# The recurrence chain's products for both heads at once, over 128 columns

## Chip, cores, metric

The kernel runs on one core of one Trainium2 chip. The metric is the device time of one execution in microseconds (us). The core's engines are TensorE (PE in the profile, its weight loads PEld), VectorE (DVE), ScalarE (ACT), GpSimd (POOL) and SyncE (SP).

## What is computed

The reference is a backbone of two layers over 512 latent and 256 context tokens of width 1024. Each layer has a mixer (differential attention, a bidirectional RWKV-7 recurrence and a short convolution, with gates) and a mixture of 16 experts. What matters here is the recurrence, run for 8 heads of size 64 in both directions, first over the context and then over the latent tokens, from the context's state:

```python
def step(s, inp):
    wt, kkt, at, kt, vt = inp[:5]
    sa = jnp.einsum('bhvk,bhk->bhv', s, kkt)
    s = s * wt[:, :, None, :] - sa[..., None] * (kkt * at)[:, :, None, :] + vt[..., None] * kt[:, :, None, :]
    y = jnp.einsum('bhvk,bhk->bhv', s, inp[5]) if emit else None
    return s, y
```

In the second layer the context's outputs y are not needed.

## The kernel before

The recurrence is done in chunks of 64 tokens. Two heads make a pair (128 partitions), so there are 4 pairs, and of each 12 chunks: 4 of the context, 8 of the latent tokens. The two directions `d` are done side by side. `rwkv_phase` runs through pairs and chunks of a layer, and for each chunk calls two things.

`window` prepares a chunk three calls ahead, with nothing of the state: products of keys and rates (`kbd`, `cbd`, `kr`), the masked matrices `g.sv`, `g.sc`, `g.tok`, and by six levels of fp16 products (`nb`, `wt`, `xx`, `xt`) an approximate inverse `g.xt`. DVE's part of a level is `wt` (L736), ACT's are `xx` and `xt` (L753, L757).

`chain` (L771) takes the state and goes through the chunk in a row of dependent steps. The tile `V` holds for each head and direction the state on 64 partitions and the value rows on the other 64; the two heads have them on opposite halves. Per call:

1. the right-hand side `zz`: `g.sv` times `V`, each head by itself, two directions summed, into that head's 64 partitions of the bank `pz`;
2. `zr`, a copy of `zz` (ACT, L806), and `aa`, `g.xt` times `zr`;
3. `sa`, a copy of `aa` (L812), and `zz` again, with `g.sc` times `sa` added;
4. `zr` as `zz` less `sa` (DVE, L804), and `aa` once more, with `g.xt` times `zr` added;
5. `aa` copied into the value rows' place in `V`, a head at a time (DVE, L824), and `pss`, the next state: `g.tok` times `V`, each head by itself, into the bank `py`;
6. the next chunk's `V` from `pss` and the decayed state `sf`, a head at a time (DVE, L846; L848 at a pair's first chunk).

Where outputs are wanted (`emit`), `yy` is made beside this, `g.sv` times `V` for each head and `g.sc` times `sa`, and copied out (ACT, L854). So a product of one head has 64 weight columns and writes 64 partitions:

```python
for h, hs in enumerate(halves):
    first = self.mma(zz[hs, 0], g.sv[:, 0, h, 0], V[:, 0, h], True)
    with tc.issue_after(first.ins):
        self.mma(zz[hs, 1], g.sv[:, 1, h, 0], V[:, 1, h])
```

All matmuls of the chain are recorded at L85 (`mma`), nearly all others at L81 (`mm`). Between the chain's steps the program places other work, doled out by `fill`: the projections `pw` (weights split in a high and a low part), three matmuls of 512 or 256 columns a step, and `pa`. It gives the chain the highest priority, then the windows, then this fill. The order on each engine is then set by a scheduler that follows a timeline of its own, and every engine goes through its own list strictly in order.

Of the kernel before, what the change touches and what calls it, by code (L numbers as in the profile page):

```python
# [8 lines left out]
F32 = mybir.dt.float32  # L9
# [58 lines left out]
class Trunk:  # L68
# [570 lines left out]
    def window(self, q, n, emit, kb):  # L639
# [39 lines left out]
        for h in range(2):  # L679
            hs, ho = slice(64 * h, 64 * h + 64), slice(64 - 64 * h, 128 - 64 * h)  # L680
            v.tensor_tensor(kbd[hs, :, ho], two(q.k)[hs], t1[hs], ALU.mult)
            v.scalar_tensor_tensor(cbd[hs, :, hs], kk[hs], -1.0, t2[hs], ALU.mult, ALU.mult)
            dst = g.sv[hs, :, h, :nm]
            if n:
                f = q.f[hs, :, n - 1, None, None].to_broadcast([64, 2, nm, 64])
                nc.gpsimd.tensor_tensor(dst, kr[hs, :, :nm], f, ALU.mult)
            else:
                nc.gpsimd.tensor_copy(dst, kr[hs, :, :nm])
# [9 lines left out]
        for h in range(2):  # L698
            ho = slice(64 - 64 * h, 128 - 64 * h)
            v.tensor_tensor(g.sv[ho, :, h, :nm], ps[ho, 0, :, :nm], self.scc[ho, :, :nm], ALU.mult)  # L700
# [70 lines left out]
    def chain(self, q, n, V, emit):  # L771
# [19 lines left out]
        pz = self.psz.tile([P, 2, 2, HD], F32, name="pz", tag="z")  # L791
        zz, aa = pz[:, 0], pz[:, 1]
        self.mark()
        for h, hs in enumerate(halves):
            first = self.mma(zz[hs, 0], g.sv[:, 0, h, 0], V[:, 0, h], True)
            with tc.issue_after(first.ins):
                self.mma(zz[hs, 1], g.sv[:, 1, h, 0], V[:, 1, h])
        py = self.psz.tile([P, 2, 2, HD], F32, name="py", tag="y")
        pss, yy = py[:, 0], py[:, 1]
        sa = None  # L800
        for it in range(2):
            r = rp.tile([P, 2, HD], F32R, name="zr", tag="zr", bufs=2)
            if it:
                v.tensor_tensor(r, zz, sa, ALU.subtract)  # L804
            else:
                nc.scalar.activation(r, zz, AF.Copy)  # L806
# [3 lines left out]
            if not it:  # L810
                sa = rp.tile([P, 2, HD], F32, name="sa", tag="sa", bufs=2)
                nc.scalar.activation(sa, aa, AF.Copy)  # L812
                self.mark()
                for d in range(2):
                    self.mma(zz[:, d], g.sc[:, d, 0], sa[:, d])
                if emit:

                    firsts = []
                    for h, hs in enumerate(halves):
                        firsts.append(self.mma(yy[hs, 0], g.sv[:, 0, h, 1], V[:, 0, h], True))  # L820
                        with tc.issue_after(firsts[-1].ins):
                            self.mma(yy[hs, 1], g.sv[:, 1, h, 1], V[:, 1, h])
        for h, hs in enumerate(halves):
# [5 lines left out]
        for h, hs in enumerate(halves):  # L829
            if last:  # L830
                break
            if emit:
                with tc.issue_after(firsts[h].ins):
                    for d in range(2):
                        self.mma(pss[hs, d], g.tok[:, d, h], V[:, d, h])
            else:
                first = self.mma(pss[hs, 0], g.tok[:, 0, h], V[:, 0, h], True)
                with tc.issue_after(first.ins):
                    self.mma(pss[hs, 1], g.tok[:, 1, h], V[:, 1, h])
        if emit:  # L840
            for d in range(2):
                self.mma(yy[:, d], g.sc[:, d, 1], sa[:, d])
        if not last:
            for h, hs in enumerate(halves):
                if n:
                    v.tensor_tensor(out[hs, :, h], pss[hs], sf[hs], ALU.add)  # L846
                else:
                    v.tensor_copy(out[hs, :, h], pss[hs])  # L848
        if emit:
# [4 lines left out]
            nc.scalar.activation(ysl, yy, AF.Copy)  # L854
# [1081 lines left out]
```

## Time and profile before

| | us |
|---|---|
| median of 3 runs | 3746.64 |
| lowest, highest | 3741.66, 3747.3 |
| the profiled execution | 3755.7 |
| its span in the trace | 3753.9 |
| the recurrence phase of the first layer, about | 115 to 975 |
| the recurrence phase of the second layer, about | 2170 to 2870 |

The profile is of one execution. The page gives the busy time of each engine, and further views split it by stretch, by group of instructions, by wait, or show the instructions in order of time. A record of PE lasts longer than the time to the next one, since matmuls overlap: what a matmul costs is read from start to start. Each matmul on plain fp32 operands has two records. A form such as 128*64 128x64 f32 reads: 128 rows and 64 columns of the array, the operand that streams through has 128 partitions and 64 columns. A wait is named by the instruction that was waited for last.

### The profile page before, as it was taken

The page shows a single profiled execution, that of the slowest core. Times are in us where ns is not written, and L with a number is a line of the kernel's source. Part 1 is how long each engine was busy: PE and PEld are TensorE (multiplying, and loading weights), DVE is VectorE, ACT ScalarE, POOL GpSimd, SP SyncE. Part 2 cuts the span into 40 slices and gives each one's busy share as a digit, 9 for nine tenths or more (in the row PEclk, how much of TensorE's full clock was granted, in tenths as well). Part 3 has the DMA queues.
Part 4 walks back from the last instruction along what each step waited for, and adds up shares of the span by engine and source line. Part 5 has one row for each costly group of instructions (what it writes and reads, how often), then busy time and mean ns, then how long its engine had stood idle before and what let it go on. Part 6 is the DMA issues. An engine that isn't in the chain of part 4 may idle for free. (4 is left out here: it accounts for less than half of the span.)

```text
span 3753.9 us, 58688 instructions
## 1 busy us (share of the span) xinstructions
PE 3485.4 (93%) x22479; PEld 2313.5 (62%) x22479; DVE 2025.0 (54%) x4902; ACT 1284.2 (34%) x3145; POOL 893.0 (24%) x1181
## 2 busy tenths in 40 slices
PE   6999999999998998999999899899999989799998
PEld 4777777777987892233333467677777978633442
DVE  6787878773665461121222677878773766412122
ACT  3454444443444211111110344555553452211111
POOL 3333343332320420000000243334343312100000
PEclk9999999999999998999999899898999999899999
DMA  5312031334115435778888411111112135399998
GB/s 177 102 61 95 29 111 49 110 114 150 52 39 183 136 133 211 294 293 310 331 331 328 138 57 29 31 36 38 35 38 92 46 132 186 132 409 409 409 409 351
DMA packets 297053, 621.11 MB, mean 165 GB/s; under 512 B 19258, under 2 KB 160532, under 8 KB 296772
## 3 DMA queue, kind: packets, MB, share of 16 engines
q1 hardware_dynamic: 293028, 605.30, 44.5%
q0 software_dynamic: 1728, 6.29, 0.5%
q10 hardware_dynamic: 2016, 5.77, 0.4%
q8 instruction: 177, 2.90, 0.3%
q14 instruction: 104, 0.85, 0.1%
HBM read 584.00 MB, written 33.29 MB: 164 GB/s over the span
## 5 line engine op out<-in xcount | busy, mean ns | idle before, releaser
L81 PE MATMUL ph<-we,xin 128*64 128x512 f32 x2048 | 514.8, 607 | 7.7 <-DMA we<-in_exp_w 4.7
L81 PE MATMUL pw<-hhi,w_hi 128*128 128x512 f32 (+1 forms) x1272 | 500.0, 397 | 14.5 <-ACT w_hi L132 6.3
L81 PE MATMUL pw<-hlo,w_hi 128*128 128x512 f32 (+1 forms) x1272 | 457.3, 364 | 0.0
L81 PE MATMUL pw<-hhi,w_lo 128*128 128x512 f32 (+1 forms) x1272 | 455.9, 364 | 1.0 <-POOL w_lo L134 1.0
L134 POOL TENSOR_TENSOR w_lo<-w_raw,w_hi 128x1024 fp32r<-128x1024 f32 x124 | 302.3, 2444 | 413.4 <-ACT w_hi L132 340.9
L81 PEld LDWEIGHTS ph<-we,xin 128*64 128x64 f32 x2048 | 151.5, 139 | 330.5 <-issue 315.7
L736 DVE TENSOR_TENSOR wt<-slot,lvm 128x256 f16<-128x256 f32 x576 | 232.8, 418 | 114.3 <-PE slot L81 78.8
L81 PEld LDWEIGHTS pw<-hhi,w_hi 128*128 128x128 f32 x1272 | 245.5, 195 | 55.2 <-ACT w_hi L132 7.6
L81 PEld LDWEIGHTS pw<-hhi,w_lo 128*128 128x128 f32 x1272 | 244.9, 194 | 38.9 <-issue 3.8
L81 PEld LDWEIGHTS pw<-hlo,w_hi 128*128 128x128 f32 x1272 | 246.2, 195 | 32.8 <-issue 13.8
L132 ACT ACTIVATE w_hi<-w_raw 128x1024 fp32r<-128x1024 f32 x168 | 177.1, 1057 | 239.4 <-DMA w_raw<-in_w_in 63.3
L81 PE MATMUL py<-we,hT 128*64 128x512 f32 x1024 | 248.5, 607 | 8.0 <-DMA we<-in_exp_w 2.8
L1791 POOL TENSOR_TENSOR ylo<-y,yhi 128x512 fp32r<-128x512 f32 x28 | 35.3, 1280 | 891.6 <-ACT yhi L1790 891.6
L753 ACT ACTIVATE xx<-slot 128x256 f16<-128x256 f32 x384 | 145.7, 382 | 166.0 <-PE slot L81 154.2
L1801 DVE TENSOR_TENSOR xr<-xr,psc 128x512 f32<-128x512 f32 x144 | 90.3, 682 | 196.6 <-PE psc L81 196.4
L1718 ACT ACTIVATE sl<-ph 64x512 f32<-64x512 f32 x64 | 37.8, 590 | 451.5 <-PE ph L81 431.8
L1719 DVE TENSOR_TENSOR hid<-sl,ph 64x512 f32<-64x512 f32 x64 | 44.2, 690 | 267.2 <-ACT sl L1718 266.7
L81 PE MATMUL slot<-xt,wt 128*128 128x128 f16 x960 | 135.9, 229 | 34.8 <-DVE wt L736 34.3
L81 PEld LDWEIGHTS py<-we,hT 128*64 128x64 f32 x1024 | 70.2, 137 | 151.6 <-issue 132.7
L81 PE MATMUL pt<-w_hi,hhi 128*128 128x256 f32 x544 | 156.2, 289 | 4.8 <-ACT xk L1115 2.0
L768 POOL COPY V<-vt 64x128 f32<-64x128 f32 x192 | 58.1, 305 | 425.3 <-PE py L85 323.0
L81 PE MATMUL pt<-w_lo,hhi 128*128 128x256 f32 x544 | 155.7, 287 | 3.2 <-POOL w_lo L134 3.2
(418 smaller groups left out, 7779.9 us busy)
## 6 DMA issues: line engine op xcount, KB each, us to landing
we<-in_exp_w SPq DMA_DIRECT2D x384, 1024.0 KB
w_raw<-in_w_in SPq DMA_DIRECT2D x124, 512.0 KB
ada_w<-in_ada_w SPq DMA_DIRECT2D x96, 512.0 KB
w_raw<-in_w_branch SPq DMA_DIRECT2D x24, 512.0 KB
w_raw<-in_w_out SPq DMA_DIRECT2D x20, 512.0 KB
gd<-gt SPq DMA_DIRECT2D x24, 384.0 KB
g<-gd SPq DMA_DIRECT2D x24, 384.0 KB
gd<-gt SPq DMA_DIRECT2D x24, 256.0 KB
```

The lines of the kernel that those rows point to most:

```text
L81: return self.leg(self.nc.tensor.matmul(out, lhsT, rhs, start=start, stop=stop))
L132: nc.scalar.activation(hi, raw, AF.Copy)
L134: self.lo_eng.tensor_tensor(lo, raw, hi.bitcast(F32), ALU.subtract)
L736: v.tensor_tensor(wt, ps, self.lvm[:, :, l], ALU.mult)
L753: nc.scalar.activation(x, ps2, AF.Copy)
L768: self.nc.gpsimd.tensor_copy(t[ho, :, h], self.two(q.vt[s][ho], z0, z1))
L1718: nc.scalar.activation(sl, ph[0:64, ns], AF.Silu)
L1719: v.tensor_tensor(hid[0:64, ns], sl, ph[64:128, ns], ALU.mult)
L1791: (v if by_block else self.ylo_eng[nh]).tensor_tensor(lo, yn, hi.bitcast(F32), ALU.subtract)
L1801: v.tensor_tensor(x, x, pt, ALU.add)
```

## The change

The two heads' weights are laid side by side in `g.sv` (the head's index moves to the last place but one; `g.tok` lies so already), so that one matmul has 128 weight columns, and the moving operand is `V` of both heads, 128 columns. The result holds for each head's 64 partitions the product with both heads' values; only the blocks of a head with itself are read. The products with `g.sc` must add into the same layout, so they read `sa` twice (`both`). `pz` and `py` become a bank each. What copies `zz`, `pss` and `yy` out reads one head's block at a time: the first copy of `zz` is split between ACT and DVE, the subtraction is two on DVE, the copy of `yy` two on ACT.

```diff
--- before.py
+++ after.py
@@ -680,7 +680,7 @@
             hs, ho = slice(64 * h, 64 * h + 64), slice(64 - 64 * h, 128 - 64 * h)
             v.tensor_tensor(kbd[hs, :, ho], two(q.k)[hs], t1[hs], ALU.mult)
             v.scalar_tensor_tensor(cbd[hs, :, hs], kk[hs], -1.0, t2[hs], ALU.mult, ALU.mult)
-            dst = g.sv[hs, :, h, :nm]
+            dst = g.sv[hs, :, :nm, h]
             if n:
                 f = q.f[hs, :, n - 1, None, None].to_broadcast([64, 2, nm, 64])
                 nc.gpsimd.tensor_tensor(dst, kr[hs, :, :nm], f, ALU.mult)
@@ -697,7 +697,7 @@
                 self.mm(ps[:, t, d, :nm], lhs[:, d], kr[:, d, :nm], True, True)
         for h in range(2):
             ho = slice(64 - 64 * h, 128 - 64 * h)
-            v.tensor_tensor(g.sv[ho, :, h, :nm], ps[ho, 0, :, :nm], self.scc[ho, :, :nm], ALU.mult)
+            v.tensor_tensor(g.sv[ho, :, :nm, h], ps[ho, 0, :, :nm], self.scc[ho, :, :nm], ALU.mult)
         hi = lambda t: t.rearrange("p d m (h i) -> p d m h i", h=2)[:, :, :nm]
         if emit:
             hi = lambda t: t.rearrange("p d m (h i) -> p (d m) h i", h=2)
@@ -788,22 +788,34 @@
                     sf[hs], V[hs, :, h], fc[hs, :, None].to_broadcast([64, 2, HD]), ALU.mult
                 )
 
-        pz = self.psz.tile([P, 2, 2, HD], F32, name="pz", tag="z")
-        zz, aa = pz[:, 0], pz[:, 1]
+
+        own = list(enumerate(halves))
+        both = lambda t, d: t[:, d, None].to_broadcast([P, 2, HD])
+        pz = self.psz.tile([P, 512], F32, name="pz", tag="z")
+        zz = pz[:, 0:256].rearrange("p (d h x) -> p d h x", d=2, h=2)
+        aa = pz[:, 256:384].rearrange("p (d x) -> p d x", d=2)
+        py = self.psz.tile([P, 2, 2, 2, HD], F32, name="py", tag="y")
+        pss, yy = py[:, 0], py[:, 1]
+
+        def begin(out, lhs):
+
+            first = self.mma(out[:, 0], lhs(0), V[:, 0], True)
+            with tc.issue_after(first.ins):
+                self.mma(out[:, 1], lhs(1), V[:, 1])
+            return first
+
         self.mark()
-        for h, hs in enumerate(halves):
-            first = self.mma(zz[hs, 0], g.sv[:, 0, h, 0], V[:, 0, h], True)
-            with tc.issue_after(first.ins):
-                self.mma(zz[hs, 1], g.sv[:, 1, h, 0], V[:, 1, h])
-        py = self.psz.tile([P, 2, 2, HD], F32, name="py", tag="y")
-        pss, yy = py[:, 0], py[:, 1]
-        sa = None
+        begin(zz, lambda d: g.sv[:, d, 0])
+        sa = first = None
         for it in range(2):
             r = rp.tile([P, 2, HD], F32R, name="zr", tag="zr", bufs=2)
-            if it:
-                v.tensor_tensor(r, zz, sa, ALU.subtract)
-            else:
-                nc.scalar.activation(r, zz, AF.Copy)
+            for h, hs in own:
+                if it:
+                    v.tensor_tensor(r[hs], zz[hs, :, h], sa[hs], ALU.subtract)
+                elif h:
+                    v.tensor_copy(r[hs], zz[hs, :, h])
+                else:
+                    nc.scalar.activation(r[hs], zz[hs, :, h], AF.Copy)
             self.mark()
             for d in range(2):
                 self.mma(aa[:, d], g.xt[:, d], r[:, d])
@@ -812,46 +824,41 @@
                 nc.scalar.activation(sa, aa, AF.Copy)
                 self.mark()
                 for d in range(2):
-                    self.mma(zz[:, d], g.sc[:, d, 0], sa[:, d])
+                    self.mma(zz[:, d], g.sc[:, d, 0], both(sa, d))
                 if emit:
 
-                    firsts = []
-                    for h, hs in enumerate(halves):
-                        firsts.append(self.mma(yy[hs, 0], g.sv[:, 0, h, 1], V[:, 0, h], True))
-                        with tc.issue_after(firsts[-1].ins):
-                            self.mma(yy[hs, 1], g.sv[:, 1, h, 1], V[:, 1, h])
-        for h, hs in enumerate(halves):
+                    first = begin(yy, lambda d: g.sv[:, d, 1])
+        for h, hs in own:
             v.tensor_copy(V[hs, :, h], aa[hs])
         if emit:
             sa = rp.tile([P, 2, HD], F32, name="sa", tag="sa", bufs=2)
             nc.scalar.activation(sa, aa, AF.Copy)
         self.mark()
-        for h, hs in enumerate(halves):
-            if last:
-                break
-            if emit:
-                with tc.issue_after(firsts[h].ins):
-                    for d in range(2):
-                        self.mma(pss[hs, d], g.tok[:, d, h], V[:, d, h])
-            else:
-                first = self.mma(pss[hs, 0], g.tok[:, 0, h], V[:, 0, h], True)
-                with tc.issue_after(first.ins):
-                    self.mma(pss[hs, 1], g.tok[:, 1, h], V[:, 1, h])
+        tok = lambda d: g.tok[:, d]
+        if last:
+            pass
+        elif emit:
+            with tc.issue_after(first.ins):
+                for d in range(2):
+                    self.mma(pss[:, d], tok(d), V[:, d])
+        else:
+            begin(pss, tok)
         if emit:
             for d in range(2):
-                self.mma(yy[:, d], g.sc[:, d, 1], sa[:, d])
+                self.mma(yy[:, d], g.sc[:, d, 1], both(sa, d))
         if not last:
-            for h, hs in enumerate(halves):
+            for h, hs in own:
                 if n:
-                    v.tensor_tensor(out[hs, :, h], pss[hs], sf[hs], ALU.add)
+                    v.tensor_tensor(out[hs, :, h], pss[hs, :, h], sf[hs], ALU.add)
                 else:
-                    v.tensor_copy(out[hs, :, h], pss[hs])
+                    v.tensor_copy(out[hs, :, h], pss[hs, :, h])
         if emit:
             s, z0, z1, nch = seg_chunks(n)
             if n % 4 == 0 and n < 8:
                 q.y[s] = rp.tile([P, 2, nch, HD], F32, name="y", tag=f"y{s}")
             ysl = self.two(q.y[s].rearrange("p d c x -> p (d c) x"), z0, nch + z1)
-            nc.scalar.activation(ysl, yy, AF.Copy)
+            for h, hs in own:
+                nc.scalar.activation(ysl[hs], yy[hs, :, h], AF.Copy)
         return out
 
     def readout(self, q, s):
```


The scheduler orders the program anew. PE's list around the end of the second chunk of the first layer; `py<-V,tok` is `pss`, `pz<-V,sv` is `zz`, `py<-V,sv` and `py<-sa,sc` are `yy`, `pw` is fill, `slot` is of the windows. Before:

```order
L81 MATMUL slot_584<-wt,xt 128x128
L85 MATMUL py<-V,tok 64x64 x2
L81 MATMUL pw<-hhi,w_hi 128x512
L81 MATMUL pw<-hlo,w_hi 128x512
L81 MATMUL pw<-hhi,w_lo 128x512
L81 MATMUL pw<-hhi,w_hi 128x512
L81 MATMUL pw<-hlo,w_hi 128x512
L85 MATMUL py<-V,tok 64x64 x2
L85 MATMUL py<-sa,sc 128x64 x2
L81 MATMUL pw<-hhi,w_lo 128x512
```

and now:

```order
L81 MATMUL slot_584<-xx,nb 128x128
L85 MATMUL py<-V,tok 128x128 x2
L81 MATMUL pw<-hhi,w_hi 128x512
L81 MATMUL pw<-hlo,w_hi 128x512
L81 MATMUL pw<-hhi,w_lo 128x512
L81 MATMUL pw<-hhi,w_hi 128x512
L81 MATMUL pw<-hlo,w_hi 128x512
L81 MATMUL pw<-hhi,w_lo 128x512
L85 MATMUL py<-sa,sc 128x128 x2
L81 LDWEIGHTS wt
```

The product for the next state stood in two places, one for each head, with five projection matmuls between; now it stands in one, and the product with `sa` some rows behind it.

DVE's list of the same call, from a window's `kbd` to the subtraction that makes `zr`. Before:

```order
L681 TENSOR_TENSOR kbd_593<-pk,t_2169 64x2x64 x2
L736 TENSOR_TENSOR wt<-slot_584,lvm 128x256
L668 TENSOR_TENSOR t_2381<-a,e_2375 128x128
L740 TENSOR_TENSOR xt<-nb,lvm 128x256
L666 TENSOR_TENSOR t_2378<-t_2378,e_2375 128x128
L670 TENSOR_TENSOR kr<-kk,e 128x2x64
L673 TENSOR_TENSOR kr<-pr,e 128x2x64
L736 TENSOR_TENSOR wt<-slot_585,lvm 128x256
L804 TENSOR_TENSOR zr<-pz,sa 128x128
```

and now, to that subtraction, which is two instructions:

```order
L681 TENSOR_TENSOR kbd_593<-pk,t_2160 64x2x64
L816 CAST zr<-pz 64x128
L681 TENSOR_TENSOR kbd_593<-pk,t_2160 64x2x64
L668 TENSOR_TENSOR t_2369<-a,e_2363 128x128
L670 TENSOR_TENSOR kr<-kk,e 128x2x64
L673 TENSOR_TENSOR kr<-pr,e 128x2x64
L183 TENSOR_TENSOR arow<-pa,arow 128x512
L666 TENSOR_TENSOR t_2366<-t_2366,e_2363 128x128
L736 TENSOR_TENSOR wt<-slot_584,lvm 128x256
L736 TENSOR_TENSOR wt<-slot_585,lvm 128x256
L1023 TENSOR_TENSOR cg<-cg,pw 128x512
L814 TENSOR_TENSOR zr<-pz,sa 64x128 x2
```

A copy of half of `zr` now stands on DVE, between the two `kbd` of a window, and the subtraction has become two.

## Rows read from the trace of the kernel before

**Rows 1.** The page, its first part: busy time, share of the span, instructions.

```profile
PE 3485.4 (93%) x22479; PEld 2313.5 (62%) x22479; DVE 2025.0 (54%) x4902; ACT 1284.2 (34%) x3145; POOL 893.0 (24%) x1181
```

**Rows 2.** Busy time by stretch: us, each engine (instructions), clock, DMA share, GB/s.

```profile
115.00:975.00 860.00, 814.49 (x6397) 642.13 (x6397) 618.52 (x1589) 384.07 (x1076) 293.72 (x430) 0.96 0.29 92
2170.00:2870.00 700.00, 646.62 (x4750) 490.40 (x4749) 519.82 (x1375) 344.05 (x970) 261.59 (x419) 0.94 0.13 39
```

**Rows 3.** PE timeline, start us, us, work: four records of 64 columns.

```profile
505.98 0.28 PE L81 MATMUL slot<-xt,wt 128*128 128x128 f16 x2
506.11 0.28 PE L81 MATMUL slot<-wt,xt 128*128 128x128 f16 x2
506.31 0.45 PE L85 MATMUL py<-V,tok 128*64 128x64 f32 x4
506.69 0.50 PE L81 MATMUL pw<-hhi,w_hi 128*128 128x512 f32 x1
507.02 0.40 PE L81 MATMUL pw<-hlo,w_hi 128*128 128x512 f32 x1
507.26 0.39 PE L81 MATMUL pw<-hhi,w_lo 128*128 128x512 f32 x1
```

**Rows 4.** PE timeline: eight records of 64 columns; fp32 of 128 columns.

```profile
500.00 0.46 PE L85 MATMUL py<-V,sv 128*64 128x64 f32 x8
500.38 0.41 PE L85 MATMUL pz<-zr,xtr 128*128 128x64 f32 x2
...
502.52 0.28 PE L81 MATMUL slot<-ident,nb 128*128 128x128 f16 x2
502.65 0.61 PE L85 MATMUL pz<-sa,sc 128*128 128x64 f32 x4
503.06 0.48 PE L81 MATMUL pw<-hhi,w_hi 128*128 128x512 f32 x1
...
508.18 0.60 PE L81 MATMUL slot<-kr,kbd 128*128 128x128 f32 x4
508.62 0.39 PE L81 MATMUL slot<-kr,cbd 128*128 128x128 f32 x2
```

**Rows 5.** PE timeline: the first and the last run of 64 columns.

```profile
115.37 0.45 PE L85 MATMUL pz<-V,sv 128*64 128x64 f32 x4
...
2849.85 0.27 PE L85 MATMUL pz<-V,sv 128*64 128x64 f32 x1
```

**Rows 6.** Groups by shape, count, busy us, mean ns, idle before: products, evacuations, cbd.

```profile
L682 DVE SCALAR_TENSOR_TENSOR cbd<-kk,t 64x128 f32<-64x128 f32 x192 | 92.2, 480 | 19.9 <-PE slot L108 17.9
...
L85 PE MATMUL pz<-V,sv 128*64 128x64 f32 x768 | 78.4, 240 | 13.6 <-DVE V L848 7.7 <-DVE V L846 5.8
...
L85 PE MATMUL py<-V,tok 128*64 128x64 f32 x704 | 74.3, 239 | 3.3 <-DVE V L824 3.2
...
L846 DVE TENSOR_TENSOR V<-py,sf 64x128 f32<-64x128 f32 x160 | 46.0, 288 | 58.6 <-PE py L85 55.8
...
L85 PE MATMUL py<-V,sv 128*64 128x64 f32 x640 | 43.6, 231 | 0.0
...
L804 DVE TENSOR_TENSOR zr<-pz,sa 128x128 fp32r<-128x128 f32 x96 | 27.1, 282 | 26.1 <-PE pz L85 16.8 <-issue 8.3 <-PE slot L81 0.4
```

**Rows 7.** Waits of PE (who, for whom, us, times, longest), 115 to 975, 2170 to 2870 us.

```profile
PE slot L81 <- DVE wt L736: 14.0, 12, 3.4
...
PE pz L85 <- DVE zr L804: 3.7, 4, 2.0
...
PE pz L85 <- DVE V L846: 2.7, 3, 2.1
...
PE slot L81 <- DVE wt L736: 22.9, 20, 2.8
PE pz L85 <- DVE V L848: 7.7, 4, 3.0
...
PE pz L85 <- DVE V L846: 3.1, 8, 0.8
```

## The prediction, before the change was run

> **What bounds the kernel now.** I read the page's busy times first, then the two stretches in which the recurrence runs, then single rows of TensorE's timeline there, and last the groups by shape and the waits. TensorE (PE) is the busiest engine, 3485.4 us, 93% of the span [rows 1]. The changed code runs only in the recurrence phase of the two layers, 115 to 975 us and 2170 to 2870 us. There PE shows 814 of 860 us and 647 of 700, VectorE (DVE) 619 and 520, ScalarE (ACT) 384 and 344 [rows 2]. So in the first layer PE is the limit, and in the second it is the limit with some slack, and DVE is second at 72% and 74%. Every PE microsecond that goes should shorten the phase, unless DVE or the dependent chain takes its place.
>
> What the busy figure hides is in the timeline. The matmuls of the chain that read V use 64 columns of the array (128*64), nearly all others 128. Take the run of four records at 506.31 [rows 3]; the profile records each fp32 matmul twice, so these are two matmuls of one head. The two fp16 records before it, at 506.11, take 0.06 us each, as the pair at 505.98 does, so the run could start at 506.23: it starts 0.08 late. The next projection matmul starts 0.38 us after the run's start, and the one behind that comes 0.33 later, where the same matmuls in a dense row follow each other in 0.24 (507.02 to 507.26): another 0.09 lost. None of these rows shows a wait. The run displaces 0.08 + 0.38 + 0.09 = 0.55 us of PE, while its four records follow each other at about 0.06. **So roughly 0.3 us goes on each change between 64 and 128 columns and back.**
>
> That this belongs to the width and not to fp32 or to V is seen beside it: at 502.65 four fp32 records of 128 columns follow two of fp16 at 0.06 each (502.52), and the projections go on 0.41 us later [rows 4], with no gap at entry.
>
> How often: in PE's timeline from the first run at 115.37 to the last at 2849.85 [rows 5] I count 369 such runs, 258 of 4 records, 71 of 8, 32 of 12 and 8 of 16. They hold the 768 + 704 + 640 = 2112 records of the three groups [rows 6]. Short runs are most, because V's halves are made one after the other and the schedule puts projections between the heads.
>
> **The change, part by part.** The chain is called 96 times (2 layers, 4 pairs, 12 chunks); 80 calls emit outputs, 88 hand on a state. So there are 96 + 80 + 88 = 264 products with V.
>
> (a) Removed: 1056 matmuls of 64 columns over 64 in 369 runs. A run of 4 costs 0.55 by the row above. A run of 8 holds both heads in the two column halves at once and also lasts 0.38 to the next start, 500.00 to 500.38 [rows 4], so 0.55 as well with entry and exit. For the 40 longer runs I add four more records at 0.06 and take 0.8. The sum is 258 x 0.55 + 71 x 0.55 + 40 x 0.8 = 213 us.
>
> (b) Added: 528 matmuls of 128 columns over 128. The trace has this very shape in the window's products: four records of 128x128 fp32 from 508.18 to 508.62, 0.44 us [rows 4]. 264 x 0.44 = 116 us. Gain of (a) and (b): 97.
>
> (c) The two products with sa and sc stream 128 columns in place of 64, by reading sa twice. Four records of 128x64 take 0.41 us (502.65 to 503.06) and of 128x128 0.44: the load of 128 weight columns paces both. 176 products x 0.03 = 5 us; between ends of 0 and 176 x 0.2 (twice the streaming, if nothing hid it) = 35 I take 5, as both rows are of the phase itself. Net gain on PE 92.
>
> (d) Evacuations become one per head. An operation on 64 partitions takes as long as one on 128: V at 64x128 0.288 us, zr at 128x128 0.282 [rows 6]. DVE gets the second half of the first residual (96 x 0.288 = 28 us) and one more subtraction a call (28 us): 56 us more, 1138 to 1194 us. ACT keeps one half at the same time and gets one more copy of y in 80 calls, at 0.28 as well 22 us; it is half idle, and nothing of the chain reads y. I put ACT at nothing: its cover is that idle half.
>
> (e) The chain grows: the second subtraction 0.29 us, and the products with V now wait for both halves where the first head could start early, then 0.44 instead of the second head's 0.23, twice: about 0.7 us a call, 67 us over all if PE ever had nothing else. It has: windows ahead and projections fill in between, and a call takes 860/48 = 17.9 us or 700/48 = 14.6 us in the two layers. So the chain's own length costs nothing while they last. What it does cost shows in PE's waits [rows 7]. For DVE's chain work PE waited 3.7 us (zr, L804) and 2.7 (V, L846) in the first layer, and 7.7 (V, L848) and 3.1 (V, L846) in the second, 17 us for three hops. One more DVE hop (the half copy) and one longer (the subtraction) I price at two such, rounded down to 10 us. For wt, the window's DVE step, it waited 14.0 and 22.9, 37 us. DVE's idle share falls from 27% (1138 of 1560) to about 20% (1194 of 1490); if that wait grows in proportion, 37 x 27/20, it is 13 us more. Ends: 0 and the 56 us of (d) in full.
>
> (f) In the second layer PE is idle for 700 - 647 = 53 us, so part of what the runs cost there lay where PE would have waited anyway. I take 9 us off. The work queued per chain call is the same in both orders; POOL's and DVE's writes of sv only change their strides and are put at nothing.
>
> Sum: -97 + 5 + 10 + 13 + 9 = **-60 us**. The profiled execution took 3755.7 us (span 3753.9), 9 more than the median of 3746.6; on the median's footing the forecast is **3687 us**.
>
> **A rule against it.** The row at 500.00 [rows 4] has eight records of two heads in the 0.38 us of the four at 506.31 [rows 3]: two column halves run side by side, and without the gap of 0.14 at its end the eight take 0.24, two at a time at 0.06. Were that what every product with V costs now, 264 x (0.44 - 0.24) = 53 us would be added; rival (4) works that out. The Trainium skill (TensorE: Matmul & The Clock Gate, "Packing small matmuls") recommends just this, putting narrow outputs on different column groups so that they run concurrently, and so speaks against the change. The trace agrees with it for the 71 runs of 8, and not for the 258 where a head stands alone and pays both changes of width.
>
> **The rivals.** (1) *DVE takes PE's place in the second layer.* It has 520 us of DVE work in 700 us; with 28 more, and in-order queues, a shorter phase may not be had. For: PE's largest wait there is for DVE's wt [rows 7]. Against: in the first layer PE hardly waits with DVE at 72%. The second layer has 190 of the 369 runs, so half of 92, 46 us, is lost, and 23 are given back: -92 + 46 + 23 = -23, 3724 us. (2) *The gaps are not the width's* but come with every start on V and stay: 264 x 0.3 us remain of 369 x 0.3, a gain of 32 less 28 given back, -4: 3743. Against: the projection behind a run waits for nothing and still loses time. (3) *Slower: PE stands at the product with xt for the half copy on DVE.* The copy is queued behind window work there: for one, the two cbd of 0.48 us each [rows 6]. If PE had to stand 1.3 us a call, 96 x 1.3 = 125 us against the other terms' -70 makes +55, 3802. It decides from 70/96 = 0.7 us a call. Against: the like subtraction costs PE 4 us in 96 calls now [rows 7]. (4) *Slower: the two halves run side by side in most runs*, and 128 columns only double the streaming: 53 + 5 + 10 + 13 = 81 us more, 3828. The 258 runs of one head speak against it.
>
> **Chances.** Forecast 0.62, (1) 0.21, (2) 0.08, (3) 0.06, (4) 0.03. A measurement can tell about 0.2% (the three runs spread 5.6 us), 7.5 us. The forecast and (1) are faster, (2) is the same: faster 0.83, same 0.08, slower 0.09. The range takes the whole PE gain of 97 at its lower end (3650, and 5 more for the counts) and (1) with 14 us of DVE's 56 on top at its upper end: 3645 to 3738.
>
> **What would show it.** Right: no 128*64 rows in the chain; 528 matmuls with V following at 0.11 us a record with no gap before or behind; both phases shorter, the first by some 40 us, the second by 20 to 40; DVE near 80% in them. Rival (1): the second phase as long as before, PE waiting for wt. Rival (3): PE's wait for the half copy of zr tens of microseconds. I am wrong if a gap of 0.1 us stays at these products, or if stages outside the phases change by more than 10 us.

## The result, and the profile after

The changed kernel takes 3780.42 us, the median of 4 runs (3776.97 to 3785.91), beside 3746.97 for the kernel before on the same chip: a ratio of 1.0091 [1.0072, 1.0109]. It is slower by 33 us where 60 less was forecast. The profiled execution took 3779.88 us, 24 more than that of before, with a span of 3778.1.

The page, its first part, answers to [rows 1]:

```profile
PE 3443.8 (91%) x21423; PEld 2314.1 (61%) x21423; DVE 2094.5 (55%) x5094; ACT 1308.8 (35%) x3225; POOL 891.6 (24%) x1181
```

PE has 42 us less to do and 1056 records fewer, and the kernel takes longer. The busy time by stretch, in the columns of [rows 2]; the second stretch is 25 us longer than there, because the phase is:

```profile
115.00:975.00 860.00, 791.62 (x5881) 645.73 (x5880) 655.42 (x1691) 396.42 (x1126) 293.98 (x437) 0.97 0.29 91
2170.00:2895.00 725.00, 625.65 (x4222) 487.16 (x4221) 553.82 (x1467) 354.12 (x1000) 259.55 (x417) 0.92 0.12 37
```

PE is idle for 68 us of the first stretch where it was for 46, and for 99 of the second where it was for 53. The granted clock goes from 0.96 to 0.97 in the first stretch and from 0.94 to 0.92 in the second. Over whole runs it is a little lower, 0.9515 at the median of the changed kernel's runs where the kernel before has 0.956; what that is worth is said with the fourth group of experiments. The length of the phase itself is read from the products of `zr` with `xt`: count, ns (shortest, median, longest), first and last start. Of before, for each layer:

```profile
L85 PE MATMUL pz<-zr,xtr x192: 192/277/423, 161.1 to 905.4; 128*128 128x64 f32 x192
L85 PE MATMUL pz<-zr,xtr x192: 193/277/402, 2233.3 to 2859.2; 128*128 128x64 f32 x192
```

and of after:

```profile
L85 PE MATMUL pz<-zr,xtr x192: 192/277/422, 156.1 to 900.8; 128*128 128x64 f32 x192
L85 PE MATMUL pz<-zr,xtr x192: 192/277/421, 2227.1 to 2883.3; 128*128 128x64 f32 x192
```

From first to last start, the first layer's chain took 744.3 us and takes 744.7 (it begins 5.0 us sooner), the second's 625.9 and now 656.2. All that PE saved is gone in the first layer, and 30 us more in the second.

The groups by shape of after answer to [rows 6]; the last column is the idle time of the engine ahead of the group and what ended it:

```profile
L85 PE MATMUL pz<-zr,xtr 128*128 128x64 f32 x384 | 76.9, 283 | 37.3 <-DVE zr L814 19.8 <-DVE zr L816 17.2
...
L85 PE MATMUL pz<-V,sv 128*128 128x128 f32 x384 | 66.6, 297 | 24.3 <-DVE V L852 21.0 <-DVE V L854 2.6 <-ACT sa L835 0.2
...
L85 PE MATMUL py<-V,tok 128*128 128x128 f32 x352 | 63.4, 305 | 11.3 <-DVE V L832 10.6
...
L814 DVE TENSOR_TENSOR zr<-pz,sa 64x128 fp32r<-64x128 f32 x192 | 54.8, 285 | 20.4 <-PE pz L85 17.7 <-PE slot L81 0.8
...
L85 PE MATMUL py<-V,sv 128*128 128x128 f32 x320 | 51.1, 283 | 0.0
...
L816 DVE CAST zr<-pz 64x128 fp32r<-64x128 f32 x96 | 28.3, 294 | 22.7 <-ACT zr L818 20.0
...
L818 ACT ACTIVATE zr<-pz 64x128 fp32r<-64x128 f32 x96 | 25.8, 269 | 15.9 <-PE pz L85 14.0
```

The first of these rows, in the kernel before:

```profile
L85 PE MATMUL pz<-zr,xtr 128*128 128x64 f32 x384 | 77.6, 285 | 6.2 <-DVE zr L804 4.2 <-ACT zr L806 1.9
```

PE stands 37.3 us ahead of the products with `zr`, where it stood 6.2. The row to remember is that of L816: the half copy on DVE waited 20.0 us for **ACT's half copy**, not for PE.

PE's waits over the two stretches answer to [rows 7] (for whom, us, times, longest):

```profile
PE slot L81 <- DVE wt L736: 14.1, 14, 2.6
PE pz L85 <- DVE V L852: 9.7, 18, 2.4
PE pz L85 <- DVE zr L816: 8.2, 5, 4.2
PE pz L85 <- DVE zr L814: 7.1, 11, 1.4
...
PE slot L81 <- DVE wt L736: 39.6, 32, 3.7
PE pz L85 <- DVE zr L814: 12.8, 15, 2.0
PE pz L85 <- DVE V L852: 11.3, 24, 0.8
...
PE pz L85 <- DVE zr L816: 9.1, 11, 2.0
```

All of these are waits for DVE. The wait for `wt` in the second layer rose from 22.9 to 39.6.

**Where the gaps went.** PE's timeline of after, at a product of 128 columns (start, us):

```profile
506.45 0.27 PE L108 MATMUL slot<-ident,cbd 128*128 128x128 f32 x1
506.56 0.27 PE L108 MATMUL slot<-ident,kbd 128*128 128x128 f32 x1
506.67 0.61 PE L85 MATMUL py<-V,sv 128*128 128x128 f32 x4
507.12 0.28 PE L81 MATMUL slot<-xx,nb 128*128 128x128 f16 x2
507.20 0.39 PE L85 MATMUL pz<-zr,xtr 128*128 128x64 f32 x2
```

It follows the record ahead of it in the same 0.11 us as that one its own, its four records take 0.45, and the next product goes on 0.08 later. The gap of 64-column runs [rows 3] is not there.

**What stands in their place.** All engines of after in the second layer, at the first copy of `zz`; in brackets the idle time ahead and what ended it:

```profile
2370.83 0.66 PE L85 MATMUL pz<-V,sv 128*128 128x128 f32 x4
...
2371.33 0.56 PE L81 MATMUL slot<-kr,cbd 128*128 128x64 f32 x4
2371.53 0.27 ACT L818 ACTIVATE zr<-pz 64x128 fp32r<-64x128 f32 x1 [0.28 <-PE pz L85]
...
2371.83 0.30 DVE L816 CAST zr<-pz 64x128 fp32r<-64x128 f32 x1 [0.45 <-ACT zr L818]
```

Both halves of `zz` were ready at 2371.5. ACT copies its half until 2371.80; DVE is free, stands for 0.45 us, and begins at 2371.83. The second way in which the halves come apart, some 27 us later:

```profile
2398.49 0.27 ACT L818 ACTIVATE zr<-pz 64x128 fp32r<-64x128 f32 x1
...
2399.24 0.42 DVE L736 TENSOR_TENSOR wt<-slot,lvm 128x256 f16<-128x256 f32 x1
...
2401.64 0.74 DVE L736 TENSOR_TENSOR wt<-slot,lvm 128x256 f16<-128x256 f32 x2
...
2402.11 0.40 PE L81 MATMUL slot<-xt,wt 128*128 128x128 f16 x2 [1.59 <-DVE wt L736]
...
2402.30 0.28 DVE L666 TENSOR_TENSOR t<-t,e 128x128 f32<-128x128 f32 x1
...
2402.70 0.29 DVE L816 CAST zr<-pz 64x128 fp32r<-64x128 f32 x1
...
2403.05 0.63 PE L85 MATMUL pz<-zr,xtr 128*128 128x64 f32 x2
```

Here ACT is done at 2398.76 and DVE comes to its half at 2402.70, behind windows and a normalisation. Over all 96 calls I set the start of the DVE half against the end of the ACT half: it never starts before it, the least distance is 32 ns, 33 calls lie within 60 ns, the mean is 0.94 us. From the start of the first half to the end of the second a call needs 1.50 us on average; in the kernel before this was one copy on ACT, 96 times 278 ns.

To see all that PE lost, I took its start-to-start times in each layer, from the first product for `zz` to the last of `zr` with `xt`, charged every record what its shape takes in a dense row, and put the excess to the change of width where neighbours differ in columns, otherwise to what ended the wait. This is a grouping of my own, good to some microseconds; in us, both layers:

| kernel | stretch | width | wt | zr | V | sc |
|---|---|---|---|---|---|---|
| before | 1462.5 | 111 | 45 | 7 | 0 | 7 |
| after | 1487.0 | 16 | 65 | 45 | 47 | 13 |
| split_only | 1508.9 | 113 | 60 | 38 | 0 | 0 |
| state_wide | 1448.6 | 78 | 48 | 7 | 17 | 7 |
| state_out_wide | 1430.2 | 67 | 47 | 11 | 14 | 5 |
| halfcopy_act | 1426.7 | 17 | 48 | 22 | 40 | 9 |
| copies_dve | 1457.0 | 17 | 56 | 36 | 45 | 11 |

(Waits for V in before lie at entries into 64 columns, so they count as width there: by [rows 6] 13.6 and 3.3 us, some 17 of the 111.) Between before and after, 95 us of width go, and 38 on `zr`, 47 on V, 20 on `wt` and 6 on `sc` come; 7 us less of dense records and some 15 more in small groups make up the 24.5 by which the stretches grew. Outside the two stretches nothing moved: 2291.4 us and 2291.1.

### The profile page after: what moved, and what is told of

Its sections match the earlier page's. It is cut to its first block, busy times and chain, and to the rows that moved or that the text cites. A ratio compares the mean times of both kernels' runs of the same rounds, so it can differ in the third digit from the quotient of the medians.

```text
span 3778.1 us, 57006 instructions
## 1 busy us (share of the span) xinstructions
PE 3443.8 (91%) x21423; PEld 2314.1 (61%) x21423; DVE 2094.5 (55%) x5094; ACT 1308.8 (35%) x3225; POOL 891.6 (24%) x1181
## 5 line engine op out<-in xcount | busy, mean ns | idle before, releaser
L81 PE MATMUL pt<-w_hi,hlo 128*128 128x256 f32 x544 | 154.9, 285 | 0.0
```

The costliest lines, as they stand in the source:

```text
L81: return self.leg(self.nc.tensor.matmul(out, lhsT, rhs, start=start, stop=stop))
```

## The experiments

The question was which part of the change costs the time: the wide products, which wait for both heads; DVE's added work; or the way in which the first `zr` is split between two engines. All ratios below are to the kernel before, run beside each, with the 95% interval.

### First: one part at a time

**split_only** is the kernel before with its narrow products, and only `zr` made per head, as in the change:

```diff
-            if it:
-                v.tensor_tensor(r, zz, sa, ALU.subtract)
-            else:
-                nc.scalar.activation(r, zz, AF.Copy)
+            for h, hs in enumerate(halves):
+                if it:
+                    v.tensor_tensor(r[hs], zz[hs], sa[hs], ALU.subtract)
+                elif h:
+                    v.tensor_copy(r[hs], zz[hs])
+                else:
+                    nc.scalar.activation(r[hs], zz[hs], AF.Copy)
```

> The kernel before with one thing of the change: zr is made a head at a time (first copy half on ACT, half on DVE; the subtraction two on DVE). All matmuls keep 64 columns. Theory A (the change gains some 94 us on PE, and the split zr on DVE, which is in the chain, gives back more): slower than before by 60 to 125 us, and PE waits for DVE's zr tens of us. Rival B (the give-back comes from wide products that must wait for V of both heads): within 10 us of before. Rival C (the scheduler's new order as such costs the time, whatever is changed): slower by about 30 without a longer wait for zr.

3796.81 us, 1.0139 [1.0094, 1.0184]: the split alone costs 49 us, less than the 60 at which theory A began, with no product touched (the 56 us that it adds to DVE are in that). Its groups show the same wait as the changed kernel's:

```profile
L85 PE MATMUL pz<-zr,xtr 128*128 128x64 f32 x384 | 79.7, 291 | 29.9 <-DVE zr L805 14.8 <-DVE zr L807 13.3
...
L807 DVE CAST zr<-pz 64x128 fp32r<-64x128 f32 x96 | 28.3, 294 | 31.3 <-ACT zr L809 29.1
```

**state_wide** makes only the product for the next state (`pss`) 128 wide, which adds no evacuation, as `out` was already made per head:

```diff
-        for h, hs in enumerate(halves):
...
-                        self.mma(pss[hs, d], g.tok[:, d, h], V[:, d, h])
...
+                for d in range(2):
+                    self.mma(pss[:, d], g.tok[:, d], V[:, d])
...
-                    v.tensor_tensor(out[hs, :, h], pss[hs], sf[hs], ALU.add)
+                    v.tensor_tensor(out[hs, :, h], pss[hs, :, h], sf[hs], ALU.add)
```

> The kernel before with only the next state pss over 128 columns; nothing is added on DVE or ACT. Removed are 160 runs of 64 columns at 0.55 us (88 us), added 88 products at 0.44 (39 us). A: faster by 30 to 49 us. B: pss now waits for both V copies, so the gain is given back: within 10 us of before or slower. C: slower by about 30.

3732.20 us, 0.9966 [0.9943, 0.9988], 15 us faster: between what A and B gave.

**state_out_wide** widens `yy` too, with its copy in two on ACT; `zz` and `zr` stay as before:

```diff
-                    for h, hs in enumerate(halves):
-                        firsts.append(self.mma(yy[hs, 0], g.sv[:, 0, h, 1], V[:, 0, h], True))
...
+                    firsts.append(self.mma(yy[:, 0], g.sv[:, 0, 1], V[:, 0], True))
...
-            nc.scalar.activation(ysl, yy, AF.Copy)
+            for h, hs in enumerate(halves):
+                nc.scalar.activation(ysl[hs], yy[hs, :, h], AF.Copy)
```

> The kernel before with pss and yy over 128 columns, the right-hand side zz still a head at a time; DVE gets nothing more, ACT one more copy of y. A: faster than before by 45 to 70 us, and faster than state_wide. B: no faster than before. C: slower by about 30.

3730.03 us, 0.9956 [0.9938, 0.9974], 17 us faster, where A had 45 to 70. Both widenings gain, but less than the gaps that they remove: the table has 33 and 44 us less of width, and 17 and 14 of new waits for V.

**halfcopy_act** is the changed kernel with the half copy of DVE moved to ACT:

```diff
                 elif h:
-                    v.tensor_copy(r[hs], zz[hs, :, h])
+                    nc.scalar.activation(r[hs], zz[hs, :, h], AF.Copy)
```

> The changed kernel with the second half of zr's first copy on ACT in place of DVE; two instructions on ACT, one DVE instruction a call less. A: 20 to 60 us less than the changed kernel's 3780, PE's wait for that copy gone. B and C: within 10 us of 3780.

3719.77 us, 0.9933 [0.9914, 0.9952]: 27 us faster than before, and 61 faster than the changed kernel, by one line. Its groups:

```profile
L85 PE MATMUL pz<-zr,xtr 128*128 128x64 f32 x384 | 76.2, 281 | 18.0 <-DVE zr L814 16.2 <-ACT zr L816 0.6 <-ACT xtr L757 0.2
...
L816 ACT ACTIVATE zr<-pz 64x128 fp32r<-64x128 f32 x96 | 26.2, 273 | 1.1
L818 ACT ACTIVATE zr<-pz 64x128 fp32r<-64x128 f32 x96 | 25.8, 269 | 17.4 <-PE pz L85 16.5
```

The two halves one after the other on one engine take 0.55 us a call, and PE's 17.2 us for L816 have become 0.6. The place of the half copy is what turns the gain into a loss. Two explanations remained: it is 28 us of work on a loaded DVE, or it is a wait of one engine for another.

### Second: load on DVE, and ways to take it off

**halfcopy_load** gives DVE its 64x128 back in halfcopy_act, as an addition that nobody reads; **before_load** puts the same two lines into the kernel before:

```diff
                 nc.scalar.activation(sa, aa, AF.Copy)
+                idle = rp.tile([P, 2, HD], F32, name="idle", tag="idle")
+                v.tensor_tensor(idle[0:64], sa[0:64], sa[0:64], ALU.add)
```

> halfcopy_act (3720, the half copy of zr on ACT) with an operation of the same form size added on DVE in every call at the chain's priority, the sum of sa with itself on 64 partitions into a tile that nobody reads. It gives DVE back about the work that the half copy was, but outside the chain. Theory A1 (DVE's load: 28 us of work on DVE cost about 60 wherever they stand): back to 3765 to 3790. Theory A2 (the place in the chain: PE stands for the half copy behind other DVE work): within 15 us of 3720.

> The kernel before with the added DVE operation of halfcopy_load (0.28 us a call, 64 partitions of sa, nobody reads it). A: with the width gaps still on PE, 27 us of load outside the chain cost less than the 25 to 29 that they cost in halfcopy_load: 5 to 25 us over before's 3747, and clearly less than split_only's 49. C: anything from -20 to +40.

halfcopy_load takes 3745.00 us, 0.9997 [0.9987, 1.0007], 25 more than halfcopy_act: between what A1 and A2 gave. before_load takes 3774.14, 1.0071 [1.005, 1.0093], 24 more than the before of its batch (3749.64). The rows of the added instruction, of halfcopy_load and of before_load:

```profile
L826 DVE TENSOR_TENSOR idle<-sa 64x128 f32<-64x128 f32 x96 | 36.3, 379 | 18.2 <-ACT sa L824 17.7
```

```profile
L814 DVE TENSOR_TENSOR idle<-sa 64x128 f32<-64x128 f32 x96 | 37.6, 391 | 22.9 <-ACT sa L812 22.6
```

Most of them take 0.28 us, as the half copy does, but a few last up to 2.5 us, so that they sum to 36 and 38 us. So DVE work with neither product nor reader costs about two thirds of its length in either kernel. But it is not load alone: ahead of it DVE stood 17.7 and 22.6 us for ACT's `sa`, about as long as the half copy stood for ACT's half. So these two runs, each in one order, give load 25 of the 60 at most.

Three edits meant to relieve DVE did not bring that back. **halfcopy_vcopy_act** and **before_vcopy_act** move the second head's copy of V to ACT:

```diff
-            v.tensor_copy(V[hs, :, h], aa[hs])
+            (nc.scalar.copy if h else v.tensor_copy)(V[hs, :, h], aa[hs])
```

> halfcopy_act with the second of the two copies of aa into V moved from DVE to ACT, where it can run beside the first. A1: another 28 us off DVE, 30 to 60 us faster, 3660 to 3690. A2: that copy is in the chain too and no longer stands behind the first on DVE, so 10 to 40 us faster. If neither (PE is the limit again, ACT's queue is the wait): within 10 us of 3720.

> The kernel before, with the same copy moved to ACT and all products at 64 columns. If DVE's work in the chain cost time before the change as well (A1 or A2): 15 to 50 us faster than 3747. If PE with its width gaps was the limit then, as the prediction had it: within 10 us of 3747.

3746.14 us, 0.9999 [0.9989, 1.0008], and 3751.30, 1.0018 [1.0008, 1.0028]: DVE has less to do, and they are slower than their own bases by 26 and 5. Each makes one more pair on the bank of `pz`: ACT's copy of `aa` never starts before DVE's has ended, the least distances are 34 and 33 ns. **fold** takes the subtraction from DVE altogether: POOL subtracts the identity from `sc`, and both copies of `zr` lie on ACT in both rounds:

```diff
+        nc.gpsimd.tensor_tensor(
+            g.sc[:, :, 0], g.sc[:, :, 0], self.ident[:, None].to_broadcast([P, 2, P]), ALU.subtract
+        )
...
-                if it:
-                    v.tensor_tensor(r[hs], zz[hs, :, h], sa[hs], ALU.subtract)
-                elif h:
-                    v.tensor_copy(r[hs], zz[hs, :, h])
-                else:
-                    nc.scalar.activation(r[hs], zz[hs, :, h], AF.Copy)
+                nc.scalar.activation(r[hs], zz[hs, :, h], AF.Copy)
```

> halfcopy_act with the subtraction taken off DVE: POOL takes the identity from sc once a window (0.7 us of POOL), so that the product with sa subtracts it as well, and zr is copied by two ACT instructions both times. DVE loses two instructions a call, 55 us. A1: 60 to 110 us faster than 3720. A2: 10 to 40 faster. If ACT's added 55 us in the chain weigh as much as DVE's: no faster than 3720.

3737.74 us, 0.9978 [0.9969, 0.9988]: a miss, 18 us slower than halfcopy_act. PE no longer waits for DVE's `zr`, but by the same count as in the table for `wt` 74 us where halfcopy_act had 48. Nor is DVE relieved by 55 us: by the pages its busy time goes from 2045.4 to 2037.8 us only, because `cbd` takes 108.4 us in place of 89.2 and `kbd` 88.3 in place of 75.8. POOL does 75 us more here, and in halfcopy_act the 96 `cbd` that lie mostly beside an instruction of POOL take 647 ns, the other 96 take 282. **half_sub_act** is halfcopy_act with the second head's subtraction replaced by a copy on ACT (it leaves out the subtraction of `sa` for that head):

```diff
-                if it:
+                if it and not h:
```

> halfcopy_act with the second head's zr of the second round copied by ACT in place of the subtraction on DVE. It leaves out the subtraction of sa for the second head. A: one DVE operation a call less in the chain, like the step from the changed kernel to halfcopy_act: 20 to 60 us under 3720. If ACT's added copy in the chain weighs as much, or C: within 15 us of 3720, or above.

3725.97 us, 0.9936 [0.992, 0.9953]: no gain over halfcopy_act, though DVE has 27 us less. With the load as the only reason it should have gained. But it makes a new pair too: in the second round ACT's copy never starts before DVE's subtraction has ended (least distance 33 ns).

### Third: the pair

**mirror** exchanges the halves, so that DVE copies the first head and ACT the second:

```diff
-                elif h:
+                elif not h:
```

> The changed kernel with the two halves of the first zr copy exchanged between the engines: the first head's on DVE, the second's on ACT. Every engine has the same work at the same place; the scheduler alone orders it otherwise. Theory A (DVE's part of the split zr costs the time, by its load and by its place in the chain): within 12 us of 3780. Rival C (the new order as such decides, and moves the time by tens of microseconds): more than 20 us away from 3780 on either side.

3760.11 us, 1.0023 [1.0012, 1.0035]. The order turns round with the edit: now ACT's half never starts before DVE's has ended, the least distance is 33 ns and the median 34, and the time lies 20 below the changed kernel, just past the line set for rival C. The one that is written second waits for the other, whichever engine it is.

**rhs_wide** is the complement of state_out_wide: `zz` wide with the split of `zr`, `pss` and `yy` narrow.

> The changed kernel with pss and yy a head at a time again, 64 columns; only the right-hand side zz is over 128 columns, with the split zr on ACT and DVE. A, by adding up: before 3747, plus 49 for the split (split_only), less 10 to 30 for zz's gaps: 3765 to 3790, slower than before. If the split is harmless and pss and yy were what cost the time: 3720 to 3750.

3780.66 us, 1.0097 [1.0072, 1.0122]: this third of the change alone loses as much as the whole of it.

### Fourth: how much of this is the order?

Any edit makes the scheduler order the program anew, so I gave four kernels another order by a number that adds no instruction, the planner's allowance of fill ahead of the chain (**before_shift**, **after_shift**, **halfcopy_shift**, **state_out_shift**):

```diff
-            self.fills = ((40.0, 6.0), (30.0, 3.0))[l]
+            self.fills = ((43.0, 6.0), (33.0, 3.0))[l]
```

> The kernel before with 3 us more of projections placed ahead of the chain in each layer; no work is added or removed, but half of PE's list comes in another order. It measures what order alone does. If the change itself is slower: all versions move by at most 12 us under this edit. If the order decides (mirror moved the changed kernel by 20): 10 to 25 us from 3747 on either side.

> The changed kernel with the same shift. If the loss comes from what the change adds on DVE: 3755 to 3790, over before_shift. If 3780 was an unlucky order alone: at or under before_shift.

> halfcopy_act with the same shift. If the half copy on DVE is what turned the gain to a loss: 20 to 60 us under after_shift, and under before_shift. If 3720 was a lucky order: at before_shift or above.

> state_out_wide with the same shift. If widening without DVE work gains some 15 us: 5 to 30 us under before_shift. If not: within 5 us of it or above.

| kernel | first order | second order | second order to before in its first [95%] | granted clock, first and second |
|---|---|---|---|---|
| before | 3748.46 | 3740.17 | 0.998 [0.9965, 0.9996] | 0.956, 0.958 |
| changed | 3780.42 | 3762.43 | 1.0039 [1.0026, 1.0053] | 0.9515, 0.956 |
| halfcopy_act | 3719.77 | 3702.12 | 0.9875 [0.9854, 0.9897] | 0.958, 0.964 |
| state_out_wide | 3730.03 | 3699.07 | 0.9859 [0.9834, 0.9883] | 0.957, 0.9645 |

A neutral edit moved these by 8, 18, 18 and 31 us, where I had allowed 12. So a difference of 20 or 30 between two kernels, each in one order, is not to be read; the misses above (fold, half_sub_act, the copies of V, mirror against after) are of this size. What holds in both orders: the change costs 33 and 22 us, the half copy on DVE in place of ACT costs 61 and 60, and widening state and output alone gains 17 and 41 (30 at most was expected in the second). state_out_shift is the fastest of all runs, and beats both kernels.

The last column, medians of the runs, shows what moved along: TensorE spent less time at the lower of its two levels (1.2 in place of 2.4 GHz) in every second order. Of the 98 runs of the kernel before that stand beside the experiments, six had a clock of 0.953 and took 3754.7 us on average, five had 0.959 and took 3740.2: 2.4 us for a thousandth. By that, which is an estimate, some 5, 11, 14 and 18 of the 8, 18, 18 and 31 us go with the clock; so do 11 of the 33 us that the change costs, and 16 and 19 of the 61 and 60 of the half copy. What lowers the clock of a kernel is not shown; in the changed kernel PE stood idle for longer in both stretches (68 and 99 us, in before 46 and 53).

### Fifth: load or wait

**copies_dve** tells the two apart. The first `zr` is copied by DVE alone, both halves: the wait for ACT is gone, and DVE has 27 us more to do than in the changed kernel:

```diff
-                elif h:
-                    v.tensor_copy(r[hs], zz[hs, :, h])
                 else:
-                    nc.scalar.activation(r[hs], zz[hs, :, h], AF.Copy)
+                    v.tensor_copy(r[hs], zz[hs, :, h])
```

> The changed kernel with both halves of the first zr copy on DVE, so one DVE operation a call more and one ACT operation less than the changed kernel. In the changed kernel's trace DVE's half never starts before ACT's half has ended: the two read the same bank of PSUM and one waits for the other, and DVE stands idle for it with the window's work queued behind. Theory A3 (that wait across the two engines is what costs most, not DVE's load): in spite of 27 us more on DVE no slower than 3780, 3755 to 3780. Theory A1 (DVE's load, at the 25 us that such an operation cost in halfcopy_load and before_load): 3795 to 3810.

> The same in the second order, that of after_shift (3762). A3: 3735 to 3762. A1: 3780 to 3795.

3752.23 us, 1.0012 [1.0002, 1.0021], and in the second order 3716.15, 0.9907 [0.9891, 0.9924]: 28 and 46 us faster than the changed kernel in the same order, with more on DVE, and faster than A3 had it. (The granted clock is 0.9575 and 0.963, by the estimate above worth some 14 and 17 of these.) Its rows:

```profile
L85 PE MATMUL pz<-zr,xtr 128*128 128x64 f32 x384 | 76.0, 281 | 28.5 <-DVE zr L814 14.2 <-DVE zr L816 13.2 <-ACT xtr L757 0.3
...
L816 DVE CAST zr<-pz 64x128 fp32r<-64x128 f32 x192 | 54.9, 286 | 13.6 <-PE pz L85 11.1
```

The copies now wait for PE's product alone, follow each other 14 ns apart, and take 0.59 us a call in place of 1.50. Load alone would have made this kernel slower. By the table its stretches are 30 us shorter than the changed kernel's, 9 of them on `zr` and 9 on `wt`. So the pair on two engines is a cost of its own. Load and DVE's queue without a pair are seen beside halfcopy_act: 55 us of copies on DVE in place of ACT cost 32 and 14 us in the two orders, so the half copy's 28 us some 16 and 7 (an estimate, half of that each), and the pair has the larger part of the 60.

## Why the prediction was wrong

- **(a), (b): right.** The width was the reason for the gaps, and they went. By the table's count PE's records and changes of width together fell by 102 us, where (a), (b) and (c) had -92; without the 17 us of waits for V in the width of before it is some 85. Rival (2) falls with the rows at 506.67, rival (4), by which PE's work would have grown, with this count.
- **(c): right.** The four records of `pz<-sa,sc` follow in 0.45 us in after (496.80 to 497.25 in its timeline), where 0.44 was taken.
- **(d): sizes right, and here the prediction failed.** DVE's two groups came to 28.3 and 54.8 - 27.1 = 27.7 us, 56 as said. The step that failed reads "ACT keeps one half at the same time". It was not at the same time. The two instructions read one bank of PSUM, and DVE's half waits for ACT's. I read their durations and added them up, one beside the other, and never asked what the second waits for. The half copy on DVE, in place of a second one on ACT, costs 61 and 60 us in the two orders. The trace of before had the sign. There ACT's second copy of `aa` (`sa`, L827) reads the bank beside DVE's copies into V (L824), and in 80 of 80 calls it starts after them, 34 ns or more:

```profile
L827 ACT ACTIVATE sa<-pz 128x128 f32<-128x128 f32 x80 | 22.1, 277 | 36.0 <-DVE V L824 32.4 <-PE slot L81 3.0 <-PE pw L81 0.5
```

- **(e): wrong in kind and size.** "One more DVE hop" was priced like the three hops of [rows 7], at 10 us together with the longer one. The hop is not of that sort: it depends on another engine, and DVE works in order, so while it stands, 20.0 us in all, the windows queued behind it stand too. PE's idle time ahead of the products with `zr` rose from 6.2 to 37.3 us, and its wait for `wt` in the two stretches by 17, where 13 was forecast. Also in (e), "the chain's own length costs nothing while they last": V of both heads before a product starts cost 47 us by the table, part of which had lain inside the entries before; state_wide, without any split, has 17 of it. So even without the half copy (halfcopy_act) the change gained 27 and 38 us in the two orders, not 60.
- **(d), DVE at its own price: open.** The sum took 13 of DVE's 56 us, from the wait on `wt`: a share of idle time, about a quarter, taken for slack. before_load and halfcopy_load lose 24 and 25 us for 36 to 38 of DVE work, standing for ACT included. The copies of copies_dve, which stand for no other engine but PE, cost 32 and 14 us for 55. So 13 for 56 was low in one order and about right in the other.
- **The rivals.** (1), DVE in PE's place, had the second layer as long as before; it is 30 us longer, and the first is not shorter either. (3), slower by the half copy on DVE, was right in its place and sign: the row at 2402.70 is the queue that it describes. But it named the queue of window work alone, and priced it at 0.7 us a call to decide; what it left out is the wait for ACT. It had a chance of 0.06, because I held the subtraction on DVE to be "the like". The subtraction follows `sa`, which ACT had finished 0.87 us or more before in every call.

**Why the halves are serial.** The Trainium skill (PSUM — Partial Sum Buffer, "PSUM bank collisions raise a hardware error") says that two engines may be in one bank at once if they are in different quadrants of 32 partitions, and that guarding by bank is the simple version. The halves here lie on partitions 0 to 63 and 64 to 127, so by that page they could run together. The traces show them apart in 96 of 96 calls, with either engine first: what ends DVE's standing is ACT's instruction, so the program orders them, whether the chip needs it or not. At L827 the two engines write different tiles, `V` and `sa`, so there it is what they read that orders them, not what they write; their partitions overlap there, though. A bank for each half, or a program that lets them overlap, was not tried.

**What stays open.** How the 60 us of the half copy divide between load (25 at most by two runs, 16 and 7 by another estimate) and the pair (the rest) is known only to the 20 or 30 us by which orders differ, and how much of either comes by way of the granted clock only by an estimate. Why the copy of V on ACT and half_sub_act gave nothing back is not settled; a new pair is in each. Nor is how much of the wait for V a better order could hide: state_out_wide gained 17 in one order and 41 in another, where its gaps were worth 44.

## What to carry to other kernels

When a change trades PE time for one more evacuation, put all pieces of a PSUM bank on one engine, or show in a trace that the second piece starts before the first ends; an in-order engine that stands for another one holds up everything queued behind it. Do not take the idle share of the second-busiest engine for slack: here 55 us of copies cost 32 us in one order and 14 in another. Before you read differences of 1%, run each kernel in a second order made by a neutral edit, and compare the granted clocks of the runs: here such an edit moved the time by up to 36 us, a good part of it with the clock.

## What was not expected of the hardware and the program

- Two half copies of one bank by ACT and DVE never overlapped (in the changed kernel the least distance is 32 ns, the mean 0.94 us); two on DVE follow 14 ns apart, two on ACT 11 to 12.
- An instruction on DVE that nobody reads (0.28 us for most, 36 and 38 us for all 96) costs 25 and 24 us of 3750, standing for ACT included, in two kernels in which DVE was busy for 55 and 54% of the span without it.
- An edit that adds no instruction moved five kernels by 8 to 36 us (copies_dve by 36), all of them down, and the granted clock up in each (by 0.002 to 0.0075).
